# A transformer block kernel: SyncE's queue in the text's order, input halves on ScalarE's queue, x loaded into unused places, and a denser plan for expert weights

## The chip, the cores and the metric

The kernel runs on one core of a Trainium2 chip. The core has TensorE (PE in the rows; PEld is its loading of stationary operands), VectorE (DVE), ScalarE (ACT), GpSimd (POOL) and SyncE (SP), and 16 DMA engines that all the DMA queues share. The metric is the device time of one execution in microseconds (us), and lower is better. The profile of one execution gives the span from the first to the last instruction, which is a little shorter than the device time.

## What is computed

One layer of a streaming encoder over 256 tokens of width 2048, all in float32: a norm, one wide input projection, two parallel mixers (sparse attention with 8 heads, and RWKV-7 with 16 heads), an output projection, and then a mixture of 16 experts, of which each token takes two.

```python
h = rms_norm(x, g_mix[l])
proj = h @ w_in[l]
...
y_dsa = dsa_mixer(q, k, v, q_idx, k_idx, w_idx, q_gain[l], k_gain[l])
y_rwkv = rwkv7_mixer(r, d_w, kr, vr, d_a, d_g, ...)
x = x + jnp.concatenate([y_dsa, y_rwkv], axis=-1) @ w_out[l]
x = x + hier_moe(rms_norm(x, g_ffn[l]), ...)
```

Inside RWKV, a state per head is updated token by token (`state*w + sa*b + v*k`). The kernel does this in chunks of 64 tokens, which needs the solution of small triangular systems.

## The kernel before

The first part is one long stream of weight tasks on TensorE. A task multiplies a 128x512 piece of a weight matrix. `load_raw` brings two such pieces (512 KB) into one of three raw places (RA's two halves and RB) with a DMA on SyncE's queue. `split` then makes a high part (a cast on ACT, L222) and a remainder (a subtraction on DVE, L223), in one of four half buffers W2, and TensorE multiplies three times with the high and low parts of the input (`hT`, or later `yT`). A column task (`add_cm`) is 12 matmuls of 256 columns, a row task (`add_tm`) 6 of 512 columns. `drive` runs the stream: loads are asked for up to 8 tasks ahead, splits 4 tasks ahead.

Between the tasks stand the matmuls of the small chains: the eight RWKV blocks (`rwkv_early`, `solve`, `solved`, `rwkv_late`), the attention, the norm (`spread`). A planner, the class `Order`, decides where: it adds up an estimated TensorE time `od.t`, each chain gives a delay with `yield`, and a step is taken when its due time has come. The table `Y` and the constants `SOLVE_US` and `RSTD_US` hold these delays, and `PACE` the rate at which weights of the experts are asked for while the stream runs. TensorE's instructions keep this order (`manual_schedule`). The order on the other engines, and on SyncE's queue, is decided by the framework's scheduler.

At the start, `xT` (the input, transposed, in four quarters of 512 KB; the first in two halves) and the first raw weights are loaded on SyncE's queue; ACT and DVE make `hT` from `xT` with the gain. The factor 1/rms of a token is needed only when the first projected blocks leave PSUM: `spread` loads x (four pieces of 512 KB, on POOL's queue) into the places of `yr` and `qT`, squares them on ACT into `vt`, and a matmul into `rps` (12 tasks into the stream) spreads the result over the partitions as `rsB`.

`solve` of an RWKV block sends its triangular systems through DRAM to POOL, which solves them row by row (`tt`, `xt`, L692 and L694) and writes `dout`; `solved` loads the result into `XT` with four DMAs on SyncE's queue (L702), and the first matmuls `pz1` of `rwkv_late` read it. `load_lora` brings small weights (128 KB) on SyncE's queue too.

After the mixers, four groups of 16 tasks multiply `wo` (the output projection). During these, `prefetch_step`, `leave_rwkv` and `wo_after` load the first expert weights, in chunks of 1 MB, on POOL's queue; a one-element copy from the current W2 half holds most of them back until the stream has come that far. Then follow the routing and the experts (`experts`), with 24 chunks for each pair of experts and 8 pairs, loaded into a ring of some 23 places.

Of the kernel before, what the change touches and what calls it, by code (L numbers as in the profile page):

```python
# [17 lines left out]
P = 128  # L18
# [17 lines left out]
PACE0 = 8.0  # L36
PACE, SOLVE_US, RSTD_US = 2.2, 39.0, 16.1
Y = [8.0, 5.6, 9.8, 1.6, 4.0, 2.6, 4.8, 5.8, 3.1, 6.0, 5.2, 3.0, 3.0, 3.1, 19.0, 5.7, 12.6, 4.4, 7.2, 4.8, 2.2, 6.6, 2.8, 6.2, 7.2, 2.2, 3.5, 0.0, 1.5, 1.1, 2.2, 16.1, 5.0, 2.2, 10.7, 10.4, 1.0, 5.0]

STREAM = ["r1", "d0", "r2", "d1", "r3", "d2", "r4", "r5", "d4", "r6", "r7", "d3", "d5", "d6", "d7"]

# [89 lines left out]
def block_kernel(ctx: ExitStack, tc: tile.TileContext, a: dict, dbg=None):  # L133
# [23 lines left out]

    ACT.preload_act_table_set("natural_log_exp_and_others")

    const = ctx.enter_context(tc.tile_pool(name="const", bufs=1))  # L160
# [13 lines left out]
    order = ExitStack()  # L174
    order.enter_context(tc.manual_schedule(engines={mybir.EngineType.PE}))

# [79 lines left out]
    with tc.tile_pool(name="xload", bufs=1) as xp:  # L256
# [4 lines left out]
        def load_xT(q, r0, r1):  # L261
            SP.dma_start(out=xT[q][:, r0:r1, :], in_=a["xT"][:, 4 * q + r0:4 * q + r1, :])

# [24 lines left out]
    def spread():  # L288

        yield 4.0  # L290
        part = const.tile([P, 2, 2], F32, name="part")
        xv = a["x"].rearrange("(j p) (c m) -> p j c m", p=P, c=2)
        xs = [t.rearrange("p b t -> p (b t)").rearrange("p (c m) -> p c m", c=2) for t in (yr, qT)]
        for j in range(2):
            for c in range(2):
                POOL.dma_start(out=xs[j][:, c, :], in_=xv[:, j, c, :])
                yield 1.0
        for j in range(2):
            for c in range(2):
                ACT.activation(out=vt[:, j, :], in_=xs[j][:, c, :], func=AF.Square, accum_out=part[:, j, c:c + 1])  # L300
                yield 1.0 * c
        DVE.tensor_tensor(out=rstd, in0=part[:, :, 0], in1=part[:, :, 1], op=ALU.add)
# [252 lines left out]
    def rwkv_early(b):  # L555
# [142 lines left out]
    def solved(b):  # L698

        yield SOLVE_US  # L700
        for ci in range(4):
            tc.keep_in_program_order(SP.dma_start(out=XTs[b % SB][32 * ci:32 * ci + 32, :, 32 * ci:32 * ci + 32], in_=dr[b][1][ci].rearrange("u s t -> s u t")))  # L702
        od.event(f"solved{b}", Y[37])

    def rwkv_late(b):
# [60 lines left out]
        for n in range(1, 3):  # L766
# [871 lines left out]
```

## Time and profile before

| what | value |
|---|---|
| device time, median of 3 runs | 1052.73 us (1046.85 to 1052.93) |
| device time of the profiled execution | 1053.52 us |
| its span | 1051.7 us |
| mean granted clock of TensorE, share of full speed | 0.998 |
| TensorE busy | 1012.2 us (96%) |
| VectorE, ScalarE, GpSimd busy | 528.9, 387.7, 257.8 us |
| moved by DMA | 298.75 MB, mean 284 GB/s |

A row of the timeline gives the start in us from the span's start, the time in us, engine, line, operation, what is written and read, and in square brackets the idle time of the engine before it with what ended it. SPq is SyncE's queue; its rows are issues of DMAs, not transfers. A row of the chain of waits gives start and length, and "DMA RB<-wo" there is a transfer from its issue to its landing. A row of the waits names the engine that waited, what it waited for, the us in total, how often, and the longest.

### The profile page before, as it was taken

The page shows a single profiled execution, that of the slowest core. Times are in us where ns is not written, and L with a number is a line of the kernel's source. Part 1 is how long each engine was busy: PE and PEld are TensorE (multiplying, and loading weights), DVE is VectorE, ACT ScalarE, POOL GpSimd, SP SyncE. Part 2 cuts the span into 40 slices and gives each one's busy share as a digit, 9 for nine tenths or more (in the row PEclk, how much of TensorE's full clock was granted, in tenths as well). Part 3 has the DMA queues.
Part 4 walks back from the last instruction along what each step waited for, and adds up shares of the span by engine and source line. Part 5 has one row for each costly group of instructions (what it writes and reads, how often), then busy time and mean ns, then how long its engine had stood idle before and what let it go on. Part 6 is the DMA issues. An engine that isn't in the chain of part 4 may idle for free.

```text
span 1051.7 us, 17181 instructions
## 1 busy us (share of the span) xinstructions
PE 1012.2 (96%) x6476; PEld 683.2 (65%) x6476; DVE 528.9 (50%) x1155; ACT 387.7 (37%) x836; POOL 257.8 (25%) x645
## 2 busy tenths in 40 slices
PE   5899999999999999999999899999999999999995
PEld 5898888889889877788877544444444444444432
DVE  5696787698978765756554313131312222221303
ACT  5666656566566754566454101010101010000001
POOL 3206676572664737002222110000000000000000
PEclk9999999999999999999999999999999999999999
DMA  8556744535454464648899798999999999999995
GB/s 286 211 180 174 203 150 136 167 114 147 134 155 139 137 189 133 235 123 289 285 324 378 314 365 352 422 419 420 420 421 419 421 420 420 419 421 420 420 405 176
DMA packets 69210, 298.75 MB, mean 284 GB/s; under 512 B 17184, under 2 KB 20048, under 8 KB 45056
## 3 DMA queue, kind: packets, MB, share of 16 engines
q1 hardware_dynamic: 54864, 248.59, 63.6%
q0 software_dynamic: 8928, 47.41, 12.7%
q10 hardware_dynamic: 5328, 1.58, 0.6%
q8 instruction: 53, 0.87, 0.3%
q14 instruction: 37, 0.30, 0.1%
HBM read 294.37 MB, written 3.15 MB: 283 GB/s over the span
## 4 chain that ended last, share of the span: by engine, by line
PE 78%; DVE 8%; DMA 5%; ACT 3%; issue 2%; POOL 2%; SPq 0%; ACTq 0%; DVEq 0%; POOLq 0%
PE pp L146 27%; PE pd L146 11%; PE gate L146 11%; PE up L146 10%; PE misc L146 6%; PE sc L146 3%; DVE W L223 3%; PE pz L146 2%; DMA RB<-wo 2%; PE py L146 2%; DMA RB<-wr 1%; POOL xt L694 1%; ACT W L222 1%; POOL tt L692 1%; DMA xT<-xT 1%
## 5 line engine op out<-in xcount | busy, mean ns | idle before, releaser
L146 PE MATMUL pp<-W,hT 128*128 128x512 f32 x768 | 190.1, 397 | 0.0
L146 PE MATMUL pp<-hT,W 128*128 128x256 f32 x1296 | 170.9, 289 | 11.8 <-DVE W L223 8.4
L223 DVE TENSOR_TENSOR W<-RA,W 128x512 fp32r<-128x512 f32 x200 | 138.3, 701 | 81.6 <-ACT W L222 80.9
L146 PEld LDWEIGHTS pp<-hT,W 128*128 128x128 f32 x1296 | 161.8, 194 | 16.2 <-DVE W L223 9.2
L222 ACT CAST W<-RA 128x512 fp32r<-128x512 f32 x200 | 121.8, 618 | 100.9 <-PE pp L146 52.2
L146 PEld LDWEIGHTS pp<-W,hT 128*128 128x128 f32 x768 | 139.8, 188 | 29.0 <-issue 0.7
L692 POOL TENSOR_TENSOR tt<-xt,at 128x24 f32<-128x24 f32 (+23 forms) x248 | 87.5, 353 | 52.5 <-DMA at<-din 33.7
L694 POOL TENSOR_TENSOR xt<-xt,tt 128x24 f32<-128x24 f32 (+23 forms) x248 | 94.4, 381 | 19.5
L146 PE MATMUL pp<-W,yT 128*128 128x512 f32 x384 | 91.3, 394 | 2.1 <-DVE W L223 2.1
L223 DVE TENSOR_TENSOR W<-RB,W 128x512 fp32r<-128x512 f32 x100 | 69.1, 696 | 48.3 <-ACT W L222 48.1
L146 PE MATMUL pd<-ew,R 128*64 128x512 f32 (+1 forms) x368 | 81.3, 580 | 2.0 <-DVE Y L1482 1.4
L222 ACT CAST W<-RB 128x512 fp32r<-128x512 f32 x100 | 61.2, 618 | 59.1 <-PE pp L146 28.3
L146 PEld LDWEIGHTS pp<-W,yT 128*128 128x128 f32 x384 | 71.0, 188 | 18.4 <-DVE W L223 3.6
L146 PE MATMUL up<-ew,R 128*64 128x512 f32 x352 | 79.3, 592 | 0.0
L146 PEld LDWEIGHTS misc<-sel,uu 128*128 128x128 f32 x512 | 60.1, 191 | 18.8 <-issue 13.8
L1491 ACT ACTIVATE Y<-pd,sv 128x512 fp32r<-128x512 f32 x31 | 21.3, 688 | 134.0 <-PE pd L146 134.0
L146 PE MATMUL misc<-sel,uu 128*128 128x128 f32 x512 | 64.9, 280 | 2.8 <-DVE R L1396 2.1
L1501 DVE TENSOR_TENSOR x<-x,sc 128x512 f32<-128x512 f32 (+1 forms) x58 | 36.2, 666 | 57.3 <-PE sc L146 57.3
L1396 DVE TENSOR_TENSOR R<-misc,gF 128x512 f32<-128x512 f32 x28 | 19.4, 692 | 87.1 <-PE misc L146 87.1
L146 PE MATMUL gate<-ew,R 128*64 128x512 f32 x272 | 61.7, 595 | 0.0
L1492 DVE SCALAR_TENSOR_TENSOR Y<-pd,sv,Y 128x512 fp32r<-128x512 f32 x31 | 23.3, 751 | 73.2 <-ACT Y L1491 73.2
L1420 ACT CAST selT<-misc 128x256 fp32r<-128x256 f32 x8 | 3.0, 372 | 153.7 <-PE misc L146 153.7
(389 smaller groups left out, 1216.4 us busy)
## 6 DMA issues: line engine op xcount, KB each, us to landing
ew<-we SPq DMA_DIRECT2D x66, 1024.0 KB, 19.9
ew<-wdn SPq DMA_DIRECT2D x38, 1024.0 KB, 19.3
ew<-we POOLq DMA_DIRECT2D x25, 1024.0 KB, 7.5
ewh<-we SPq DMA_DIRECT2D x24, 1024.0 KB, 18.2
RA<-wd SPq DMA_DIRECT2D x43, 512.0 KB, 3.8
RA<-wr SPq DMA_DIRECT2D x35, 512.0 KB, 3.9
RB<-wd SPq DMA_DIRECT2D x21, 512.0 KB, 3.7
RA<-wo SPq DMA_DIRECT2D x21, 512.0 KB, 4.6
```

What stands on the lines that cost most here:

```text
L146: PE.matmul(out, lhsT=lhsT, rhs=rhs, start=start, stop=stop, skip_group_check=skip)
L222: ACT.copy(out=hi, in_=raw)
L223: DVE.tensor_tensor(out=lo, in0=raw, in1=hi.bitcast(F32), op=ALU.subtract)
L692: POOL.tensor_tensor(out=tv, in0=xt[:, 0:n, s_:s_ + 1].broadcast_to([P, n, m]), in1=at[s_ >= 8][:, s_ % 8 if s_ < 8 else s_ - 8, s_ + 1:32 ...
L694: POOL.tensor_tensor(out=xt[:, 0:n, s_ + 1:32], in0=xt[:, 0:n, s_ + 1:32], in1=tv, op=ALU.subtract)
L1396: DVE.tensor_tensor(out=t[:, a:b], in0=ps.rearrange("p (a t) -> p a t", t=P)[:, a:b], in1=gF[:, 4 * kq + a:4 * kq + b].rearrange("p (a o) ...
L1420: ACT.copy(out=selT, in_=ps[:, 0:T])
L1491: ACT.activation(out=yh, in_=pd, func=AF.Copy, scale=sv[:, 1:2])
L1492: DVE.scalar_tensor_tensor(out=yl, in0=pd, scalar=sv[:, 1:2], in1=yh.bitcast(F32), op0=ALU.mult, op1=ALU.subtract)
L1501: DVE.tensor_tensor(out=x1[j][:, ns], in0=(uu[:, j, ns] if first else x1[j][:, ns]), in1=ps, op=ALU.add)
```

## The change

SyncE is added to the engines that keep the text's order. The loads of `xT` go to ScalarE's queue, ahead of the load of its table. `spread` loads x at the start: its fourth piece into half of `G[1]`, without any condition, the other three into buffers of the tag `MM` behind a one-element copy that reads the third quarter of `hT`; the squares are written in place. `load_lora` stands at later places in the text. In the planner, `PACE` falls from 2.2 to 1.8, `SOLVE_US` rises from 39 to 42, some delays in `Y` change, and `r4` (RWKV block 4) comes ahead of `d2` in the stream.

```diff
-PACE, SOLVE_US, RSTD_US = 2.2, 39.0, 16.1
-Y = [8.0, 5.6, 9.8, 1.6, 4.0, 2.6, 4.8, 5.8, 3.1, ..., 3.0, 3.1, ..., 12.6, ..., 5.0]
-STREAM = ["r1", "d0", "r2", "d1", "r3", "d2", "r4", "r5", ...]
+PACE, SOLVE_US, RSTD_US = 1.8, 42.0, 16.1
+Y = [8.0, 5.6, 9.8, 2.4, 4.0, 2.6, 4.8, 5.8, 3.4, ..., 3.6, 3.1, ..., 13.2, ..., 4.0]
+STREAM = ["r1", "d0", "r2", "d1", "r3", "r4", "d2", "r5", ...]
...
-    ACT.preload_act_table_set("natural_log_exp_and_others")
...
-    order.enter_context(tc.manual_schedule(engines={mybir.EngineType.PE}))
+    order.enter_context(tc.manual_schedule(engines={mybir.EngineType.PE, mybir.EngineType.SP}))
...
-            SP.dma_start(out=xT[q][:, r0:r1, :], in_=a["xT"][:, 4 * q + r0:4 * q + r1, :])
+            ACT.dma_start(out=xT[q][:, r0:r1, :], in_=a["xT"][:, 4 * q + r0:4 * q + r1, :])
...
+        ACT.preload_act_table_set("natural_log_exp_and_others")
...
-        yield 4.0
...
-        xs = [t.rearrange("p b t -> p (b t)").rearrange("p (c m) -> p c m", c=2) for t in (yr, qT)]
-        for j in range(2):
-            for c in range(2):
-                POOL.dma_start(out=xs[j][:, c, :], in_=xv[:, j, c, :])
-                yield 1.0
-        for j in range(2):
-            for c in range(2):
-                ACT.activation(out=vt[:, j, :], in_=xs[j][:, c, :], func=AF.Square, accum_out=part[:, j, c:c + 1])
-                yield 1.0 * c
+        xs = [state.tile([P, 1024], F32, name="xs", tag="MM", bufs=SB + 1) for _ in range(3)] + [G[1][:, 1024:2048]]
+        POOL.tensor_copy(xs[0][0:1, 0:1], hT[2][0:1, 0, 0, 0:1].bitcast(F32))
+        for n in range(4):
+            POOL.dma_start(out=xs[n], in_=xv[:, n // 2, n % 2, :])
+        yield 10.0
+        for n in range(4):
+            ACT.activation(out=xs[n], in_=xs[n], func=AF.Square, accum_out=part[:, n // 2, n % 2:n % 2 + 1])
+            yield 1.0 * (n % 2)
...
-            load_lora(b + 1, i)
...
-        load_lora(b + 1, 0)
         DVE.tensor_tensor(out=kd, in0=k, in1=di, op=ALU.mult)
         yield Y[2]
+        load_lora(b + 1, 0)
...
-            tc.keep_in_program_order(SP.dma_start(out=XTs[b % SB][...], in_=dr[b][1][ci].rearrange("u s t -> s u t")))
+            SP.dma_start(out=XTs[b % SB][...], in_=dr[b][1][ci].rearrange("u s t -> s u t"))
...
+        load_lora(b + 1, 2)
         od.release("@late")
```

The first place is ACT's queue from the start. hT and W are the high parts, RA and RB the raw weights; a row with x2 stands for two instructions. Before:

```order
L158 ACT_TABLE_LOAD
L285 ACTIVATE hT_68<-xT_110,gT 128x256 x2
L222 CAST W_83<-RA 128x512 x2
L285 ACTIVATE hT_68<-xT_110,gT 128x256 x2
L285 ACTIVATE hT_69<-xT_111,gT 128x256 x4
L222 CAST W_84<-RA 128x512 x2
L285 ACTIVATE hT_70<-xT_112,gT 128x256 x4
```

Now, behind the five DMAs of xT:

```order
L275 ACT_TABLE_LOAD
L284 ACTIVATE hT_67<-xT_109,gT 128x256
L220 CAST W_82<-RA 128x512
L284 ACTIVATE hT_67<-xT_109,gT 128x256 x3
L298 ACTIVATE G_88,part<-G_88 128x1024
L284 ACTIVATE hT_68<-xT_110,gT 128x256 x4
L220 CAST W_82<-RA 128x512
L284 ACTIVATE hT_69<-xT_111,gT 128x256 x4
```

The second cast of W has moved behind the second quarter of hT, and the square of the fourth piece of x (L298) stands between the first two quarters.

The second place is ACT's queue some ten us later, from the cast of RB (tasks 4 and 5 of the stream) on. Before, the squares are the L300 rows:

```order
L222 CAST W_83<-RB 128x512 x2
L498 CAST two_early<-G_89 128x256
L498 CAST lw<-lraw 128x256
L222 CAST W_84<-RA 128x512 x2
L222 CAST W_83<-RA 128x512 x2
L300 ACTIVATE vt,part<-yr 128x1024
L222 CAST W_84<-RB 128x512 x2
L300 ACTIVATE vt,part<-yr 128x1024
L300 ACTIVATE vt,part<-qT 128x1024 x2
L303 ACTIVATE rstd<-rstd,eps_t 128x2
```

Now:

```order
L220 CAST W_82<-RB 128x512 x2
L496 CAST two_early<-G_88 128x256
L496 CAST lw<-lraw 128x256
L220 CAST W_83<-RA 128x512 x2
L298 ACTIVATE xs,part<-xs 128x1024 x3
L301 ACTIVATE rstd<-rstd,eps_t 128x2
L220 CAST W_82<-RA 128x512 x2
L302 ACTIVATE rstd<-rstd 128x2
L220 CAST W_83<-RB 128x512 x2
```

The three remaining squares stand in one run ahead of the casts for tasks 8 to 11, where before one square stood behind those of 8 and 9 and three behind those of 10 and 11.

The third place is the first result of the solve. On SyncE's queue XT<-dout is that load, RA and RB are weights. Before:

```order
L210 DMA RA<-wd 128x1024 x2
L210 DMA RB<-wd 128x1024
L210 DMA RA<-wd 128x1024
L702 DMA XT_186<-dout_198 32x4x32 x4
L210 DMA RA<-wd 128x1024
L210 DMA RB<-wd 128x1024
```

Now:

```order
L208 DMA RB<-wd 128x1024
L208 DMA RA<-wd 128x1024 x2
L699 DMA XT_186<-dout_198 32x4x32 x4
L208 DMA RB<-wd 128x1024
L208 DMA RA<-wd 128x1024
L208 DMA RA<-wr 128x1024
```

The load of XT stands behind one more load of weights. On TensorE, the matmuls that read it (pz<-R,XT), with those ahead of them from the matmuls of `p3` on; before:

```order
L146 MATMUL p_1562<-con,G_89 128x128 x2
L146 MATMUL pp<-W_83,hT_68 128x512 x6
L146 MATMUL pp<-W_84,hT_68 128x512 x12
L146 MATMUL pp<-W_83,hT_69 128x512 x3
L146 MATMUL pz<-X_192,two_early 128x256 x4
L146 MATMUL pb<-Vc,AB 64x64 x8
L146 MATMUL pp<-W_83,hT_69 128x512 x6
L146 MATMUL pz_1640<-R,XT_186 128x128 x4
```

Now (ahead of the first of these rows 12 matmuls of 128x512 stand since the last 256-column task, before it were 6):

```order
L146 MATMUL p_1575<-con,G_88 128x128 x2
L146 MATMUL pp<-W_83,hT_67 128x512 x12
L146 MATMUL pp<-W_82,hT_68 128x512 x12
L146 MATMUL pb<-Vc,AB 64x64 x8
L146 MATMUL pz<-X_192,two_early 128x256 x4
L146 MATMUL pz_1647<-R,XT_186 128x128 x4
```

Since that task there are now 36 matmuls of 512 columns ahead of the reader, where there were 33. Over the eight blocks, 38, 48, 58, 68, 77, 89, 99 and 109 loads of weights stand ahead of XT before, and 39, 49, 59, 68, 77, 89, 99 and 109 now; counted in tasks of the stream, the reader comes 1.5 nearer to its load in the first block and in the third to fifth, and 1 nearer in the second. On POOL's queue, twelve chunks of expert weights instead of eleven stand ahead of the first one that no copy holds back.

## Rows read from the trace of the kernel before

**Rows 1.** The page's head and its first part: span, and TensorE's busy time, share and instructions.

```profile
span 1051.7 us, 17181 instructions
...
PE 1012.2 (96%) x6476; PEld 683.2 (65%) x6476; DVE 528.9 (50%) x1155; ACT 387.7 (37%) x836; POOL 257.8 (25%) x645
```

**Rows 2.** Busy time of the engines by stretch (PE, PEld, DVE, ACT, POOL, each with its instructions), then the granted clock of TensorE, the mean busy share of the DMA engines, and GB/s: the start, the end of the projection, and 100 us of the experts.

```profile
0.00:50.00 50.00, 35.74 (x260) 34.47 (x261) 29.44 (x61) 30.54 (x62) 16.14 (x43) 1.00 0.75 254
...
550.00:600.00 50.00, 44.52 (x248) 33.01 (x248) 21.13 (x66) 15.07 (x33) 10.59 (x22) 1.00 0.87 341
600.00:700.00 100.00, 99.16 (x514) 44.45 (x511) 22.19 (x43) 8.71 (x13) 5.80 (x11) 1.00 0.97 387
```

**Rows 3.** The waits of TensorE's matmuls over the whole span: us in total, times, longest.

```profile
PE pp L146 <- DVE W L223: 10.5, 6, 7.0
PE pp L146 <- ACT hT L285: 3.4, 1, 3.4
PE rps L146 <- DVE G L307: 2.8, 1, 2.8
PE tps L156 <- DVE re L742: 2.2, 1, 2.2
...
PE pz L146 <- DVE R L728: 1.1, 1, 1.1
...
PE pbp L146 <- DVE two_early L499: 0.8, 1, 0.8
```

**Rows 4.** The timeline of the first 36 us, chosen rows.

```profile
0.74 1.28 ACT L158 ACT_TABLE_LOAD   x1 [0.74 <-PEq L1631]
...
1.66 0.90 SPq L210 DMA_DIRECT2D RA<-wr  x2
...
5.61 0.62 ACT L222 CAST W<-RA 128x512 fp32r<-128x512 f32 x1 [0.42 <-DMA RA<-wr]
...
7.00 1.65 PE L146 MATMUL pp<-hT,W 128*128 128x256 f32 x6 [7.00 <-DVE W L223]
...
12.04 7.88 PE L146 MATMUL pp<-hT,W 128*128 128x256 f32 x42 [3.39 <-ACT hT L285]
...
15.41 3.30 ACT L285 ACTIVATE hT<-xT,gT 128x256 fp32r<-128x256 f32 x8
...
18.62 1.13 ACT L222 CAST W<-RB 128x512 fp32r<-128x512 f32 x2
...
19.78 1.06 POOL L296 DMA_DIRECT2D yr<-x  x2 [16.01 <-DMA G<-lora]
...
20.14 8.89 PE L146 MATMUL pp<-hT,W 128*128 128x256 f32 x72 [0.21 <-DVE W L223]
...
21.43 2.51 ACT L222 CAST W<-RA 128x512 fp32r<-128x512 f32 x4 [0.93 <-DMA RA<-wr]
...
28.45 1.14 ACT L222 CAST W<-RB 128x512 fp32r<-128x512 f32 x2 [2.83 <-DMA RB<-wr]
...
29.86 3.13 PE L146 MATMUL pp<-hT,W 128*128 128x256 f32 x24 [0.83 <-DVE W L223]
...
31.71 1.06 ACT L300 ACTIVATE vt<-qT 128x1024 f32<-128x1024 f32 x1
...
35.82 0.67 PE L146 MATMUL rps<-G 128*128 128x256 f32 x2 [2.82 <-DVE G L307]
```

**Rows 5.** The same columns as Rows 2 for two stretches of 3 us in the start.

```profile
6.00:9.00 3.00, 1.65 (x6) 1.35 (x6) 0.69 (x1) 0.23 (x1) 0.00 (x0) 1.00 1.03 241
...
12.00:15.00 3.00, 2.96 (x13) 2.83 (x14) 2.70 (x7) 2.62 (x7) 0.00 (x0) 1.00 1.03 411
```

**Rows 6.** The timeline where the first solve's result is loaded and read.

```profile
121.93 0.33 SPq L210 DMA_DIRECT2D RA<-wd  x1
...
122.35 1.99 SPq L702 DMA_DIRECT2D XT<-dout  x4
...
125.19 0.35 SPq L210 DMA_DIRECT2D RA<-wd  x1
...
129.64 1.05 PE L146 MATMUL pz<-R,XT 128*128 128x128 f32 x8
```

**Rows 7.** The view of the tile XT: from the issue to the landing of its 32 DMAs.

```profile
DMA to landing us min/median/max: 3.7/6.3/7.9
```

**Rows 8.** The timeline of the fifth block: the load of XT and its reader.

```profile
291.34 1.81 SPq L702 DMA_DIRECT2D XT<-dout  x4
...
301.48 0.72 PE L146 MATMUL pz<-R,XT 128*128 128x128 f32 x5
```

**Rows 9.** The chain of waits at the end of the projection: two of the last loads of wo.

```profile
557.13 7.92 DMA RB<-wo
...
567.12 9.30 DMA RB<-wo
```

**Rows 10.** The view of the DMAs: issues, KB of each, and the median from issue to landing.

```profile
RB<-wo SPq DMA_DIRECT2D x11, 512.0 KB, 4.7
```

**Rows 11.** The timeline at the same place: the last matmuls of the projection.

```profile
573.35 3.01 PE L146 MATMUL pp<-W,yT 128*128 128x512 f32 x12 [0.50 <-DVE W L223]
...
577.93 1.65 PE L146 MATMUL pp<-W,yT 128*128 128x512 f32 x6 [1.57 <-DVE W L223]
```

**Rows 12.** The waits of SyncE's queue over the whole span.

```profile
SPq L210 <- DVE W L223: 345.1, 120, 7.5
```

More of the change, by code (lines that the diff above doesn't have):

```diff
@@ L36 @@
 PACE0 = 8.0
-PACE, SOLVE_US, RSTD_US = 2.2, 39.0, 16.1
-Y = [8.0, 5.6, 9.8, 1.6, 4.0, 2.6, 4.8, 5.8, 3.1, 6.0, 5.2, 3.0, 3.0, 3.1, 19.0, 5.7, 12.6, 4.4, 7.2, 4.8, 2.2, 6.6, 2.8, 6.2, 7.2, 2.2, 3.5, 0.0, 1.5, 1.1, 2.2, 16.1, 5.0, 2.2, 10.7, 10.4, 1.0, 5.0]
-STREAM = ["r1", "d0", "r2", "d1", "r3", "d2", "r4", "r5", "d4", "r6", "r7", "d3", "d5", "d6", "d7"]
+PACE, SOLVE_US, RSTD_US = 1.8, 42.0, 16.1
+Y = [8.0, 5.6, 9.8, 2.4, 4.0, 2.6, 4.8, 5.8, 3.4, 6.0, 5.2, 3.0, 3.6, 3.1, 19.0, 5.7, 13.2, 4.4, 7.2, 4.8, 2.2, 6.6, 2.8, 6.2, 7.2, 2.2, 3.5, 0.0, 1.5, 1.1, 2.2, 16.1, 5.0, 2.2, 10.7, 10.4, 1.0, 4.0]
+STREAM = ["r1", "d0", "r2", "d1", "r3", "r4", "d2", "r5", "d4", "r6", "r7", "d3", "d5", "d6", "d7"]
 class Order:
@@ L621, in rwkv_early @@
         AB = state.tile([P, 2, 4, 64], F32, name="AB", bufs=SB)
-        MM = state.tile([P, 2, 4, 2, 64], F32, name="MM", bufs=SB + 1)
+        MM = state.tile([P, 2, 4, 2, 64], F32, name="MM", tag="MM", bufs=SB + 1)
         pas = [pbank("pa") for _ in range(2)]
@@ L701, in solved @@
         for ci in range(4):
-            tc.keep_in_program_order(SP.dma_start(out=XTs[b % SB][32 * ci:32 * ci + 32, :, 32 * ci:32 * ci + 32], in_=dr[b][1][ci].rearrange("u s t -> s u t")))
+            SP.dma_start(out=XTs[b % SB][32 * ci:32 * ci + 32, :, 32 * ci:32 * ci + 32], in_=dr[b][1][ci].rearrange("u s t -> s u t"))
         od.event(f"solved{b}", Y[37])
```

## The prediction

> **What bounds the kernel now.** I read the page's head first: TensorE is busy for 96% of the span [rows 1], so the sum can only come from its 40 us of idle time, or from new idle time. The stretches say where that lies: 14.3 of the first 50 us, 5.5 of the 50 us at the end of the projection, and under 1 us of 100 in the experts [rows 2]. The clock is at its full 2.4 GHz level in all three, so it is no term. The experts are therefore out of the sum: their chunks are in another place in the plan, but TensorE's work there is the same. That leaves the waits [rows 3]: the largest are for the split of weights (10.5 us), for hT (3.4), for the matmul of rstd (2.8) and for a few planned chains (2.2, 1.1, 0.8).
>
> The timeline of the start shows which they are [rows 4]. TensorE begins at 7.00 us, six matmuls later it waits 3.39 us for hT, at 29.86 it has waited 0.83 us for a split, and at 35.82 it has waited 2.82 us for rstd. What lies behind the last two: POOL issues x only at 19.78; the last of its squares on ACT begins at 31.71; and RB's weights keep ACT idle for 2.83 us, since they share the DMA engines with x.
>
> **The change, part by part.**
>
> *The input on ScalarE's queue.* The first weights are now issued behind one small load only. One issue on SyncE's queue is 0.45 us (0.90 for two, [rows 4]), so the first split, which follows the cast at 5.61, can be 0.45 us earlier; the table's load (1.28 us) behind five such issues ends at about 0.74 + 5 x 0.45 + 1.28 = 4.3 us, before that cast. Gain at most 0.4.
>
> The 3.39 us wait will not just go. Half a quarter of xT no longer queues behind two pieces of weights, but ACT's new order casts the second piece of W after four more hT, so TensorE stops for that instead. What counts is when the cast of RB (tasks 4 and 5) is done. Before, ACT runs without a break from 15.41 to 18.62 + 1.13 = 19.75. Best case: the 3.39 us are gained. Worst: the early piece of x, 0.5 MB, moves everything back; at the 411 GB/s of the second stretch in [rows 5] that is 1.3 us. I take a gain of 0.8 for the first five tasks, nearer the worst, as ACT also has 1.06 us more to do there, a square.
>
> *x early.* The copy that holds back three pieces reads a part of hT that is written at about 15.4, so they are issued 4.4 us before the 19.78 of now, and are 0.5 MB less (1.3 us). The last square could then begin at 31.71 - 5.7 = 26.0. Nothing waits for rstd any more, but the new order puts three squares in one run (3 x 1.06, so 3.2 us) ahead of the casts for tasks 8 and 9. If the last begins at 26.0, they end at 27.1; with a cast (0.62, as at 5.61) and a subtraction that I take to be as long, task 8 is ready at 28.4. Before, TensorE came to task 8 at about 25.9: 20.14 plus 48 matmuls of 0.12 (8.89 us for 72). With the gain of 0.8 it comes at 25.1 and waits 3.3 us. Tasks 8 to 11 then run in 5.8 us without a wait, to 34.2, against 35.82. If x lands sooner, the squares follow the first two of the casts of RA from 21.43 on (2.51 us for four), begin at 22.7, end at 25.9, and TensorE is there at 33.0. So the start as a whole gains 1.6 to 2.8; I take 2.0, with bounds at a loss of 1.3 (above) and a gain of 7.0 (3.39 + 0.83 + 2.82, all gone).
>
> *SyncE in the text's order.* Its queue waits 345 us for free raw places [rows 12], so it is ahead of what it feeds, and the small loads at later places cost and bring nothing; without that cover each would delay a load of weights by its issue, 0.33 us [rows 6]. What matters is XT. In the first block it was issued at 122.35 and read at 129.64, 7.3 us later, without a wait [rows 6]. Now it stands behind one more load, that of 125.19, so it is issued at about 125.6. The reader moves by three matmuls of 0.25 us (3.01 us for 12, [rows 11]), to 130.4, which leaves 4.8 us. A DMA of XT takes 3.7 to 7.9 us, 6.3 in the middle [rows 7], and the last one is issued some 1.5 us after the first. So TensorE waits 0.4 (if 5.2 suffices) to 2.5 us (if 7.3 are needed); I take 2.0, since the middle lies nearer to the long end. In the fifth block 10.1 us lie between them [rows 8]; 1.5 tasks less (2.2 us) leave 7.9, which is enough, and the third and fourth I take to be like it, the others keep their place.
>
> *Delays in the plan.* Three of the longer waits in [rows 3] have their delay raised: pbp 0.8 us (raised by 0.8), pz 1.1 (by 0.3), tps 2.2 (by 0.6). I count 0.8 + 0.3 + 0.6 = 1.7 as gained. Bounds: none of it, or all 4.1. The block that changes place with a projection brings the same tasks, so I count it at nothing; it is covered by the four tasks that are split ahead, and costs a wait like those three, 0.8 to 2.2 us, where a chain then comes too late.
>
> *Expert weights in closer sequence.* At the end of the projection two loads of wo take 7.92 and 9.30 us [rows 9], against 4.7 in the middle [rows 10], and TensorE waits 0.50 and 1.57 us for their splits [rows 11]. One chunk of 1 MB now goes ahead of that crowd: at 411 GB/s it is 2.5 us less there. I take a gain of 1.5, between 2.1 (both gone) and a loss of 1.0 if the denser sequence slows a load of wo earlier, where the trace shows no wait.
>
> The sum: -2.0 (start) + 2.0 (XT) - 1.7 (delays) - 1.5 (end of the projection) = -3.2 us on a span of 1051.7. Around the span of that execution lie 1053.52 - 1051.7 = 1.8 us, so the time is 1048.5 + 1.8 = 1050.3, say 1050; the median of the runs, 1052.73, is 0.8 below the profiled one.
>
> **The rivals.**
>
> First: the start gives all it has. If x is squared before TensorE comes to task 8 and the second quarter is there early, the 7.0 us go and not 2.0: 1050 - 5 = 1045. For it speaks that the ACT rows hold no long wait for DMA but those of the weights; against it that ACT has the same casts and more squares before task 8.
>
> Second: the start gives nothing, because three queues share the same engines. In the stretch from 6 to 9 us these are fully busy at only 241 GB/s [rows 5], while POOL's small loads are under way. A 0.5 MB piece on POOL's queue then delays xT by its 1.3 us, and the start loses 1.3 where I count 2.0 won: 1050 + 3.3 = 1053, so no change. The Trainium skill, DMA: Bandwidth & Descriptors, section Issuing engines are not separate DMA queues, speaks for this one: by it DMAs of several engines run on the same 16 and interleave, and only the time of issuing is saved. The busy share in that stretch agrees; no row here shows three queues at once.
>
> Third, the slower one: XT comes too late in every block. Its place is now fixed by the plan, and the plan knows nothing of how long its DMA takes. If every block had only the 4.8 us of the first, at 7.9 us per load that is 3.1 x 8 = 25 us; half of it, 12, gives 1050 + 12 = 1062. It decides from the point at which more than two blocks have under 7.3 us between issue and reader. Against it: no load of XT stands more than one load of weights later than now, and no reader comes more than 1.5 tasks nearer.
>
> **How the numbers follow.** The forecast, 1047 to 1053, gets 0.50; the first rival 0.15; the second 0.20; the third, or another chain too late, 0.15. The likeliest is the first of these, so 1050. For the range I go out to the first rival with the delays' upper bound (1045 - 2.4, so 1043) and to most of the third (1059): about 8 in 10. A measurement can tell about 1%, 10.5 us, from no change. Over 1% faster (under 1042) would need all the waits of the start, all of the delays and of the end of the projection at once: 0.10. Over 1% slower (over 1063) is the upper part of the third rival: 0.08. Within: 0.82.
>
> **What would show it.** In the changed kernel's profile: no wait of rps for DVE, and one of 2 to 4 us for a split near task 8, between 24 and 30 us; TensorE at the rstd matmul at about 34; the first block's pz preceded by up to 2.5 us of idle time that a DMA of XT ends; the last loads of wo at 6 to 8 us and under 1 us of waits for their splits. It would be wrong if ACT waits long for the first square of x at 8 to 12 us (the start then loses), if pz waits in more than two blocks, or if SyncE's queue waits for dout with weights behind it.

## The result, and the profile after

The changed kernel takes 1063.93 us (median of 4, 1060.37 to 1064.67), beside 1052.83 us of the kernel before on the same chip: ratio 1.011, 95% interval 1.0064 to 1.0155, so about 11 us slower. The profiled execution took 1064.67 us, its span is 1062.9 us.

The page's head and first part of the kernel after:

```profile
span 1062.9 us, 17143 instructions
...
PE 1016.4 (96%) x6476; PEld 688.0 (65%) x6476; DVE 527.9 (50%) x1155; ACT 387.9 (36%) x836; POOL 256.8 (24%) x646
```

Against [rows 1] the span is 11.2 us longer, and TensorE is busy 4.2 us longer with the same 6476 matmuls. So two things happened: 7.0 us more idle time, and 4.2 us because the same work ran slower. The stretches say where the clock fell (columns as in [rows 2]):

```profile
0.00:50.00 50.00, 33.64 (x235) 33.09 (x236) 27.58 (x58) 29.33 (x60) 17.21 (x44) 0.90 0.70 236
50.00:150.00 100.00, 97.17 (x706) 87.40 (x706) 78.90 (x162) 59.98 (x127) 48.26 (x124) 0.98 0.60 174
...
350.00:450.00 100.00, 96.87 (x699) 78.36 (x699) 68.64 (x160) 60.25 (x142) 50.85 (x136) 0.98 0.59 174
...
550.00:600.00 50.00, 44.58 (x239) 34.54 (x238) 21.58 (x57) 19.47 (x40) 9.93 (x21) 1.00 0.97 382
600.00:700.00 100.00, 98.21 (x519) 47.37 (x520) 22.16 (x53) 7.49 (x12) 7.36 (x14) 0.98 0.88 350
```

TensorE has 33.64 us of work in the first 50 us instead of 35.74 [rows 2], at a mean clock of 0.90. The end of the projection is as it was (44.58 and 44.52), with the DMA engines now at 0.97 of their time instead of 0.87. The waits of TensorE's matmuls over the whole span (total, times, longest):

```profile
PE pp L146 <- DVE W L221: 21.7, 6, 7.6
PE pz L146 <- DMA XT<-dout: 6.3, 4, 2.8
```

The waits for splits have doubled [rows 3], those for the load of XT are new, and the ones for hT, rstd, tps and pbp are gone.

By the place in the program: TensorE's first matmul of wo starts at 482.2 us before and 491.8 now, its last ends at 581.7 and 591.8, and the first matmul of the experts starts at 594.1 and 605.6. So 9.6 of the 11.2 us are lost ahead of the projection with wo (3.1 of them by the rstd matmul), 0.5 in it, 1.4 between it and the experts, and none in the experts.

The start, timeline of the first 40 us, chosen rows (ACTq is ScalarE's DMA queue):

```profile
0.74 3.60 ACTq L260 DMA_DIRECT2D xT<-xT  x5
...
4.38 1.28 ACT L275 ACT_TABLE_LOAD   x1 [4.38 <-DMA xT<-xT]
...
7.61 2.93 PE L146 MATMUL pp<-hT,W 128*128 128x256 f32 x12 [7.61 <-DVE W L221]
...
12.90 1.06 ACT L298 ACTIVATE G<-G 128x1024 f32<-128x1024 f32 x1 [4.87 <-DMA G<-x]
...
13.96 1.69 ACT L284 ACTIVATE hT<-xT,gT 128x256 fp32r<-128x256 f32 x4
...
15.55 0.60 ACT L220 CAST W<-RA 128x512 fp32r<-128x512 f32 x1
...
16.87 1.59 POOL L295 DMA_DIRECT2D xs<-x  x3
...
16.93 12.31 PE L146 MATMUL pp<-hT,W 128*128 128x256 f32 x84 [6.40 <-DVE W L221]
...
31.60 7.51 PE L146 MATMUL pp<-hT,W 128*128 128x256 f32 x48 [2.35 <-DVE W L221]
...
38.96 0.60 PE L146 MATMUL rps<-G 128*128 128x256 f32 x2
```

Beside [rows 4]: the table's load ends at 5.66 us, since the five issues ahead of it took 3.60 us, 0.72 for each where I had counted 0.45. Then ACT stands still for 4.87 us with the square of the early piece of x at the head of its queue; the second quarter of hT and the second piece of W are behind it. TensorE stops at 10.5 and goes on at 16.93. From there it runs at half clock, and again behind the wait of 2.35 us at 31.60 (windows of 3 and 4 us):

```profile
9.00:12.00 3.00, 1.54 (x8) 1.24 (x6) 0.00 (x0) 0.00 (x0) 0.00 (x0) 1.00 1.03 418
...
15.00:18.00 3.00, 1.06 (x5) 1.07 (x6) 2.98 (x8) 3.00 (x8) 1.37 (x4) 0.50 0.79 281
18.00:21.00 3.00, 3.00 (x16) 3.00 (x16) 3.00 (x8) 3.00 (x8) 2.25 (x3) 0.50 1.04 272
...
31.00:35.00 4.00, 3.40 (x16) 3.40 (x17) 2.75 (x6) 1.99 (x5) 0.00 (x0) 0.59 0.39 120
```

At 0.50 the clock is at its lower level, 1.2 GHz. Before the change TensorE waited 3.39 us at this place, and the clock stayed up [rows 2, 4]. The rstd matmul comes at 38.96 us instead of 35.82.

The load of XT, timeline of the first and the fifth block, and the view of the tile:

```profile
126.64 1.81 SPq L699 DMA_DIRECT2D XT<-dout  x4
...
134.70 1.62 PE L146 MATMUL pz<-R,XT 128*128 128x128 f32 x6 [2.76 <-DMA XT<-dout]
```

```profile
298.79 2.04 SPq L699 DMA_DIRECT2D XT<-dout  x4
...
308.54 1.13 PE L146 MATMUL pz<-R,XT 128*128 128x128 f32 x8 [1.61 <-DMA XT<-dout]
```

```profile
DMA to landing us min/median/max: 2.4/6.8/9.1
```

In the first block the reader could have started 5.3 us after the first issue (134.70 - 2.76 - 126.64), and the four loads took 8.1. In the fifth it is 8.1 us, and they took 9.7. Before, the reader came 7.3 and 10.1 us behind the first issue [rows 6, 8]. The other two waits stand in the fourth block (1.16 us) and the sixth (0.73). The first of the waits is followed by another stretch at half clock, and so is one for a split at 420 us (that wait, the windows behind the two, and one more between the projection and the experts):

```profile
423.02 1.20 PE L146 MATMUL pp<-W,hT 128*128 128x512 f32 x4 [2.38 <-DVE W L221]
```

```profile
134.00:137.00 3.00, 2.30 (x10) 2.23 (x11) 1.98 (x5) 0.73 (x3) 2.45 (x8) 0.52 0.42 90
424.00:427.00 3.00, 3.00 (x38) 2.02 (x39) 1.75 (x4) 0.62 (x1) 1.34 (x3) 0.54 0.95 373
...
600.00:610.00 10.00, 9.05 (x49) 6.37 (x50) 3.23 (x15) 0.17 (x1) 1.01 (x2) 0.83 0.30 106
```

In the last of these windows no wait is long: TensorE's two longest idle times there are 1.14 and 0.73 us.

At the end of the projection, the view of the DMAs (median us from issue to landing) and the last matmuls:

```profile
RA<-wo SPq DMA_DIRECT2D x21, 512.0 KB, 5.9
...
RB<-wo SPq DMA_DIRECT2D x11, 512.0 KB, 6.3
```

```profile
578.00 3.02 PE L146 MATMUL pp<-W,yT 128*128 128x512 f32 x12 [1.92 <-DVE W L221]
...
588.00 1.66 PE L146 MATMUL pp<-W,yT 128*128 128x512 f32 x6 [1.09 <-DVE W L221]
```

A load of wo into RB takes 6.3 us instead of 4.7 [rows 10]. TensorE has two waits here of 1.92 and 1.09 us, where it had 0.50 and 1.57 [rows 11]; the first of them comes four tasks earlier than the 0.50 did.

### The profile page after: what moved, and what is told of

The parts are those of the page before. It is cut to its first block, busy times and chain, and to the rows that moved or that the text cites. A ratio compares the mean times of both kernels' runs of the same rounds, so it can differ in the third digit from the quotient of the medians.

```text
span 1062.9 us, 17143 instructions
## 1 busy us (share of the span) xinstructions
PE 1016.4 (96%) x6476; PEld 688.0 (65%) x6476; DVE 527.9 (50%) x1155; ACT 387.9 (36%) x836; POOL 256.8 (24%) x646
## 4 chain that ended last, share of the span: by engine, by line
PE 66%; DMA 14%; POOL 7%; DVE 6%; issue 3%; ACT 2%; ACTq 0%; SPq 0%; POOLq 0%; DVEq 0%
PE pp L146 24%; PE gate L146 9%; PE up L146 9%; PE pd L146 8%; PE misc L146 6%; POOL tt L689 3%; POOL xt L691 3%; PE sc L146 3%; DMA XT<-dout 3%; DMA ew<-wdn 2%; DMA ew<-we 2%; DMA eww<-we 2%; PE pz L146 2%; DVE W L221 2%; DMA at<-din 2%
## 5 line engine op out<-in xcount | busy, mean ns | idle before, releaser
L691 POOL TENSOR_TENSOR xt<-xt,tt 128x24 f32<-128x24 f32 (+23 forms) x248 | 91.6, 369 | 19.5
L146 PEld LDWEIGHTS misc<-sel,uu 128*128 128x128 f32 x512 | 61.5, 195 | 18.8 <-issue 13.8
```

What stands on the lines that cost most here:

```text
L146: PE.matmul(out, lhsT=lhsT, rhs=rhs, start=start, stop=stop, skip_group_check=skip)
L691: POOL.tensor_tensor(out=xt[:, 0:n, s_ + 1:32], in0=xt[:, 0:n, s_ + 1:32], in1=tv, op=ALU.subtract)
```

## The experiments

Eighteen kernels, each timed together with the kernel before. In the table, "rstd" is the start of the rstd matmul in the profile, "XT" the waits of TensorE for the load of XT (us, times), "splits" its waits for splits from 450 to 600 us, "wo" the median landing of the loads of wo into RA and RB.

| kernel | us | ratio to before (95%) | rstd | XT | splits | wo |
|---|---|---|---|---|---|---|
| before | 1052.7 | 1 | 35.8 | 0 | 2.1, 2 | 4.6, 4.7 |
| the change | 1063.9 | 1.0110 (1.0064-1.0155) | 39.0 | 6.3, 4 | 3.0, 2 | 5.9, 6.3 |
| `s1_old_start` | 1062.9 | 1.0125 (1.0085-1.0165) | 38.1 | 5.6, 3 | 1.9, 1 | 5.6, 5.8 |
| `s2_new_start_alone` | 1055.1 | 1.0013 (0.9988-1.0039) | 39.5 | 1.8, 1 | 1.5, 1 | 5.6, 4.8 |
| `s3_square_late` | 1059.8 | 1.0090 (1.0055-1.0126) | 36.6 | 4.9, 3 | 1.9, 1 | 5.6, 5.9 |
| `s4_x_all_late` | 1063.1 | 1.0101 (1.0068-1.0133) | 35.5 | 7.2, 4 | 3.9, 3 | 5.6, 6.1 |
| `m1_old_numbers` | 1053.3 | 0.9998 (0.9975-1.0021) | 37.2 | 0.9, 2 | 0.4, 1 | 4.8, 4.8 |
| `m2_reader_later` | 1059.3 | 1.0057 (1.0032-1.0083) | 39.1 | 0.9, 1 | 5.7, 4 | 6.5, 5.8 |
| `m3_pace` | 1061.3 | 1.0086 (1.0061-1.0111) | 36.9 | 4.5, 3 | 2.0, 3 | 4.9, 4.8 |
| `m4_sp_alone` | 1052.0 | 0.9995 (0.9969-1.0022) | 34.6 | 0 | 0 | 5.1, 4.3 |
| `n1_xt_pair` | 1069.6 | 1.0138 (1.0106-1.0171) | 40.2 | 5.0, 3 | 4.1, 7 | 6.6, 6.1 |
| `n2_pace` | 1058.1 | 1.0036 (1.0013-1.0058) | 38.4 | 1.8, 2 | 3.0, 2 | 5.1, 4.9 |
| `n3_delays` | 1063.1 | 1.0082 (1.0050-1.0114) | 37.2 | 6.7, 3 | 0.7, 1 | 4.7, 4.5 |
| `n4_stream` | 1058.7 | 1.0044 (1.0020-1.0067) | 36.7 | 0.5, 1 | 1.2, 1 | 5.5, 5.1 |
| `f1_load_earlier` | 1066.3 | 1.0119 (1.0098-1.0140) | 36.8 | 2.1, 1 | 7.8, 6 | 6.5, 7.3 |
| `f2_pair_back` | 1067.6 | 1.0129 (1.0112-1.0147) | 36.6 | 5.5, 2 | 4.9, 3 | 5.4, 6.4 |
| `f3_base_square_late` | 1052.2 | 0.9990 (0.9974-1.0006) | 37.5 | 1.7, 2 | 0.3, 1 | 4.9, 4.3 |
| `f4_three_out` | 1054.7 | 1.0032 (1.0009-1.0054) | 37.3 | 1.3, 1 | 0 | 4.9, 4.5 |
| `g1_earlier_pace` | 1059.1 | 1.0064 (1.0036-1.0092) | 38.5 | 1.8, 1 | 3.0, 3 | 5.9, 5.0 |
| `g2_earlier_square` | 1064.1 | 1.0107 (1.0067-1.0146) | 36.4 | 0.2, 1 | 7.6, 7 | 6.9, 6.9 |

0.1% is 1.05 us. Differences between kernels of different rows are taken from the ratios.

### The start

My theory after reading the profile: start and middle lose apart from each other, 3 us and 8 us.

`s1_old_start`, the start's hunks reversed:

```diff
-            ACT.dma_start(out=xT[q][:, r0:r1, :], in_=a["xT"][:, 4 * q + r0:4 * q + r1, :])
+            SP.dma_start(out=xT[q][:, r0:r1, :], in_=a["xT"][:, 4 * q + r0:4 * q + r1, :])
...
-        xs = [state.tile([P, 1024], F32, name="xs", tag="MM", bufs=SB + 1) for _ in range(3)] + [G[1][:, 1024:2048]]
+        xs = [t.rearrange("p b t -> p (b t)").rearrange("p (c m) -> p c m", c=2) for t in (yr, qT)]
```

> The changed kernel with the whole start of before: xT on SyncE's queue, the table first, x on POOL's queue into yr and qT, squares into vt. Theory A (start and middle lose apart from each other, and the sum is what was measured): the rstd matmul is back at about 35.8 us instead of 38.96, the granted clock stays at its upper level in the first 40 us, the four waits of pz for XT remain, and the time is 1064 - 3.1 = 1061, or 1059 if the half-clock stretches in the start cost more on top. Rival B (the start is the whole loss, because all later chains run against a stream that is late): 1053. Rival C (the start's loss is made good later, the middle is everything): 1064.

Not so: the ratio is 1.0125, no better than the change. TensorE waits 5.2 us for rstd in it, and the middle loses as before. `s2_new_start_alone` has the same hunks the other way round, in the kernel before.

> The kernel before with the new start alone; SyncE's order, delays, stream and loads of lora as before. Theory A: the rstd matmul at about 39 us, 3 us late, and 1053 + 3 = 1056 (up to 1058). Rival B: 1064. Rival C: 1053.

1.0013: the new start costs 1.4 us at the middle of its interval, which holds zero. So the start is not where the 11 us are, although the rstd matmul is 3.7 us late in this profile too.

`s3_square_late`: the early piece stays early, its square waits.

```diff
+        one = const.tile([P, 1], F32, name="one")
+        POOL.tensor_scalar(one, hT[2][:, 0, 0, 0:1].bitcast(F32), 0.0, 1.0, ALU.mult, ALU.add)
...
-            ACT.activation(out=xs[n], in_=xs[n], func=AF.Square, accum_out=...)
+            ACT.activation(out=xs[n], in_=xs[n], func=AF.Square, scale=one if n == 3 else 1.0, accum_out=...)
```

> The changed kernel, but the square of the early piece of x also takes as its scale a column of ones that is written once the third quarter of hT is there; so the piece is still loaded early, and only its square stands later in ACT's queue. Theory A1 (the square at the head of ACT's queue is what stops the start): the second quarter of xT landed at 9.25 us, so its hT ends at about 11 instead of 15.6, TensorE's wait of 6.4 us falls to 2 or 3 with a second one for the next weights, the clock stays up, and the rstd matmul comes 2 to 3 us earlier, at 36 to 37; time about 1061. Rival A2 (the 512 KB ahead of xT are what cost): the wait of 6.4 us shrinks by less than 1.3, and the time stays at 1063.

The timeline of its start, chosen rows:

```profile
9.48 1.71 ACT L284 ACTIVATE hT<-xT,gT 128x256 fp32r<-128x256 f32 x4 [1.24 <-DMA xT<-xT]
...
12.47 1.71 PE L146 MATMUL pp<-hT,W 128*128 128x256 f32 x12 [1.74 <-DVE W L221]
...
16.14 4.02 PE L146 MATMUL pp<-hT,W 128*128 128x256 f32 x24 [1.96 <-DVE W L221]
...
36.63 0.59 PE L146 MATMUL rps<-G 128*128 128x256 f32 x2
```

As theory A1 has it, hT of the second quarter begins at 9.48 and not at 13.96, TensorE goes on at 12.47, the one wait of 6.40 us is now 1.74 and 1.96, and the clock stays at 1.00 in the first 40 us. The order in ACT's queue moved hT and shortened the wait, since the bytes are loaded as before. For the clock this isn't shown: with the square late as well, it is 0.96 in `f4_three_out` and `g2_earlier_square`. In all twelve profiles with the square early this wait is 5.2 to 6.4 us and ends at 16.6 to 17.1 us; in the four with it late TensorE goes on at 12.1 to 13.8. The Trainium skill, PSUM — Partial Sum Buffer, section Engine vs sequencer instructions, calls ScalarE's queue a strict FIFO; the 4.87 us in the timeline after agree. Most of that is spent again on the way: the rstd matmul comes at 36.6 to 40.2 us in the twelve, at 36.4 to 37.5 in the four, 1.1 us earlier on the mean. The time gains 0.2% by the ratios, less than either interval. `s4_x_all_late` holds back the piece itself:

```diff
+        POOL.tensor_copy(xs[3][0:1, 0:1], hT[2][0:1, 0, 0, 0:1].bitcast(F32))
```

> The changed kernel, but the early piece of x is held back by the same copy as the other three, so no byte of x is ahead of xT and its square is late as well. Theory A1: hardly better than the kernel in which only the square is late, 0 to 1.3 us (the 512 KB at 411 GB/s), and then a loss where the last piece of x lands later. Rival A2: all of the start's loss of 3 us is undone by this one and not by that one; 1061 against 1063.

The rstd matmul comes at 35.5, 3.5 us earlier than in the change, and the time hardly moves (1.0101): the middle gives it back, with 7.2 us for XT and 3.9 for splits.

### The numbers or the order

`m1_old_numbers` is the change with PACE, SOLVE_US, Y and STREAM of before:

```diff
-PACE, SOLVE_US, RSTD_US = 1.8, 42.0, 16.1
+PACE, SOLVE_US, RSTD_US = 2.2, 39.0, 16.1
...
```

> The changed kernel with PACE, SOLVE_US, Y and STREAM of before; SyncE in the text's order, the new places of the loads of lora and the new start stay. The new start alone cost 2 us. Theory N (the numbers lose the middle: the reader of XT stands 4 us of planned time behind its load instead of 5, and r4 ahead of d2): the waits for XT shrink to one of 2 us in the first block, the wait for W at 420 us goes, and the time is 1053 + 2 = 1055 to 1057. Theory Q (SyncE's fixed order loses it, whatever the numbers): three or four waits for XT stay, 5 to 6 us, and the time is 1061 to 1064.

0.9998. With the old numbers the loss is gone, and SyncE's order with the new start costs nothing that can be measured. No run puts the new numbers into the kernel with the old order, so whether they lose without SyncE's order isn't shown. `m4_sp_alone` is the kernel before with SyncE's order and the new places of `load_lora` (their hunks are left out here):

```diff
-    order.enter_context(tc.manual_schedule(engines={mybir.EngineType.PE}))
+    order.enter_context(tc.manual_schedule(engines={mybir.EngineType.PE, mybir.EngineType.SP}))
```

> The kernel before with SyncE's queue in the text's order and the loads of lora at their new places; start and numbers as before. Theory N: 1053, with no waits for XT. Theory Q: 5 to 6 us of waits for XT in three or four blocks, 1058 to 1060. A start that is late by 2 us at the rstd matmul, as in the kernel with the old start, is expected of either, since the squares and the casts stand as there.

0.9995, without one wait for XT: by itself the order costs nothing that can be measured. I had expected its rstd matmul late; it is early, at 34.6.

Two numbers of the change, set one at a time. `m2_reader_later` puts the reader of XT 8 us behind its load, where before the change it was 5:

```diff
-Y = [..., 4.0]
+Y = [..., 8.0]
```

> The changed kernel with one number: the reader of XT is planned 8 us behind its load instead of 4. From first issue to last landing the load took 3.8 to 9.6 us. If the waits for XT (6.3 us in four) and the stretch at half clock behind the first of them (1.7 us) are what the middle loses: no wait for XT of over 1 us, and 1064 - 8 = 1056. If the chains only end later and something else waits: 1061 to 1064.

XT is no longer waited for (0.9 us), and 5.6 us of the time come back, not 8: the splits now wait 5.7 us at the end of the projection. `m3_pace`:

```diff
-PACE, SOLVE_US, RSTD_US = 1.8, 42.0, 16.1
+PACE, SOLVE_US, RSTD_US = 2.2, 42.0, 16.1
```

> The changed kernel with PACE 2.2 as before. If the denser loading of expert weights costs at the end of the projection and where a one-element copy on POOL holds a W2 half (2.4 us at 420 us): 1064 - 2 to -4 = 1060 to 1062. If PACE is worth nothing either way: 1064.

Loads of wo are back at 4.9 and 4.8 us. By the ratios 2.5 us of the time come back too, which is less than the change's own interval.

### One number at a time on the old ones

The base is `m1_old_numbers`. `n1_xt_pair` sets SOLVE_US 42 and the reader's delay 4, `n2_pace` PACE 1.8, `n3_delays` the four raised delays, `n4_stream` puts r4 ahead of d2 (one hunk each, in this order):

```diff
-PACE, SOLVE_US, RSTD_US = 2.2, 39.0, 16.1
-Y = [..., 5.0]
+PACE, SOLVE_US, RSTD_US = 2.2, 42.0, 16.1
+Y = [..., 4.0]
...
-PACE, SOLVE_US, RSTD_US = 2.2, 39.0, 16.1
+PACE, SOLVE_US, RSTD_US = 1.8, 39.0, 16.1
...
-Y = [8.0, 5.6, 9.8, 1.6, ..., 3.1, ..., 3.0, 3.1, ..., 12.6, ...]
+Y = [8.0, 5.6, 9.8, 2.4, ..., 3.4, ..., 3.6, 3.1, ..., 13.2, ...]
...
-STREAM = ["r1", "d0", "r2", "d1", "r3", "d2", "r4", "r5", ...]
+STREAM = ["r1", "d0", "r2", "d1", "r3", "r4", "d2", "r5", ...]
```

> The changed kernel with PACE, Y and STREAM of before (1053.3 us), but SOLVE_US 42 and the reader of XT 4 us behind its load, as in the change. Theory P (this pair makes the load of XT late, and is about half of the loss): three or four waits for XT, 4 to 6 us, perhaps a stretch at half clock, and 1053 + 5 = 1058. If XT is late only together with r4 ahead of d2 or the other delays: no waits for XT, 1053.

> The same base (1053.3 us) with PACE 1.8 alone. From the run with PACE 2.2 in the changed kernel: 1053 + 2.7 = 1056, lost in waits for splits of wo, at 525 to 580 us, and not at the waits for XT. My prediction's step counted 1.5 us as gained here: 1052.

> The same base with the four raised delays alone (2.4, 3.4, 3.6 and 13.2). My prediction's step counted 1.7 us as gained: the waits pbp, pz for R and tps go, 1051.6. If chains that come later only run into others: 1053 or 1054.

> The same base with r4 ahead of d2 alone. My prediction counted it at nothing: 1053. The parts of the loss so far (XT pair and its clock 4.6, PACE 2.7, start 2.3 of 11) leave 1.5 to 3 us over; if they are here: 1055 to 1056, with waits in the blocks from 140 to 310 us.

Each costs: 1.4%, 0.4%, 0.8% and 0.5%, that is 15, 4, 9 and 5 us. Together, in the change, they cost 11. So they don't add up, and none has a price of its own. The waits of TensorE in `n1_xt_pair` and in `n3_delays`:

```profile
PE pz L146 <- DMA XT<-dout: 5.0, 3, 2.7
...
PE tps L156 <- DVE qo L879: 3.1, 1, 3.1
```

```profile
PE pz L146 <- DMA XT<-dout: 6.7, 3, 4.6
```

In `n3_delays` neither the load of XT nor its reader has another number, yet there is a wait of 4.6 us for it in the first block: 5.5 us lie between the first issue and the place of the reader, where the base has 7.4 with the same planned delay, and the reader starts 10.1 us after that issue, where the base's starts after 7.9. The other chains' delays have moved the stream against the load, and the load takes longer there. In `n4_stream` XT is not late at all, and tps waits 4.1 us.

### The load of XT on its own, and three causes together

`f1_load_earlier` leaves the reader where the change has it and asks for the load 3 us earlier; `f2_pair_back` has the pair as before the change.

```diff
-PACE, SOLVE_US, RSTD_US = 1.8, 42.0, 16.1
-Y = [..., 4.0]
+PACE, SOLVE_US, RSTD_US = 1.8, 39.0, 16.1
+Y = [..., 7.0]
```

> The changed kernel with the load of XT planned 3 us earlier and its reader where the change put it (SOLVE_US 39, delay of the reader 7: the sum is 46 as in the change). In SyncE's queue 38, 48, 58, 67, 76, 87, 99 and 110 loads of weights stand ahead of XT. The solve's result is in DRAM 4.5 us or more before the load is issued, so nothing new has to be waited for. Theory P (the lateness of the load is what the pair costs): no wait for XT over 1 us, 1064 - 6.3 - 1.7 = 1056. Theory M (any other place of the chains costs elsewhere, since the plan fits one set of numbers only): the waits for XT go, others come, 1059 to 1063.

> The changed kernel with SOLVE_US 39 and the reader 5 us behind its load, as before the change; PACE, the four delays, the stream, the start as in the change. The same loads stand ahead of XT as in the kernel with the load earlier, and the reader is planned 2 us earlier. Theory P: one or two waits for XT of 1 to 2 us, 1058. Theory M: other waits come, 1060 to 1066, as the delays alone on the old numbers cost 9 us.

My theory P fell. In `f1_load_earlier` only the first block waits for XT (2.1 us), the stream comes to the 1800th matmul of the weights 7.6 us earlier than in the change, and the kernel is no faster (1.0119). `f2_pair_back` is no faster either (1.0129), with a wait of 4.5 us for XT in the first block. In `f1_load_earlier` TensorE needs 109.0 us from the first matmul of wo to the last, where the change needs 100.0. The chain of waits at the end of the projection, and the landing of the loads of wo, show where the gain went:

```profile
509.31 9.55 DMA RA<-wo
...
539.31 8.84 DMA RA<-wo
...
550.23 8.76 DMA RA<-wo
...
561.06 9.08 DMA RA<-wo
```

```profile
RA<-wo SPq DMA_DIRECT2D x21, 512.0 KB, 6.5
...
RB<-wo SPq DMA_DIRECT2D x11, 512.0 KB, 7.3
```

```profile
PE pp L146 <- DVE W L221: 7.8, 6, 2.1
```

Loads of wo of nearly 9 us stand in that chain, and TensorE waits 7.8 us for splits. The time that was gained ahead of the projection was lost again inside it. `f4_three_out` takes PACE and the early square away as well, `g1_earlier_pace` and `g2_earlier_square` one of the two; `f3_base_square_late` is `m1_old_numbers` with the square late. For `f4_three_out`, beside the hunk of `s3_square_late`:

```diff
-PACE, SOLVE_US, RSTD_US = 1.8, 42.0, 16.1
-Y = [..., 4.0]
+PACE, SOLVE_US, RSTD_US = 2.2, 39.0, 16.1
+Y = [..., 7.0]
```

> The changed kernel without the three causes so far: square late (4.1 us in its own run), PACE 2.2 (2.7), load of XT 3 us earlier with the reader where it is (8 if theory P holds). If they add up: 1064 - 4 - 2.7 - 8 = 1049. If theory M holds: 1056 to 1060, since the four delays and r4 ahead of d2 stay.

> The changed kernel with the load of XT 3 us earlier (its reader in place) and PACE 2.2; the start as in the change. With PACE 1.8 this was 1066.3, with 8.4 us of waits for splits of wo at 517 to 580 us. If PACE is what loses the end of the projection: these waits shrink to 1 us or none, and 1066 - 8 = 1058. If the square is what the kernel with all three taken out gained: 1063 to 1066.

> The same earlier load of XT and the early square late, PACE 1.8 as in the change. If PACE loses the end of the projection: its waits stay at 5 to 8 us, and 1066 - 2 to -4 = 1062 to 1064. If the square alone brings the 11.6 us: 1055.

> PACE, SOLVE_US, Y and STREAM of before, SyncE in the text's order, the new start with the early square late. If what that square costs is the same here as in the changed kernel (there 4 us): 1053.3 - 2 to -4 = 1049 to 1051, with the rstd matmul near 36 and no half clock in the first 40 us; the one candidate that may beat both kernels. If not: 1053.

Page and loads of wo of `f4_three_out` (this profiled execution is its shortest, the median is 1054.7):

```profile
span 1048.0 us, 17137 instructions
...
PE 1014.2 (97%) x6476; PEld 686.3 (65%) x6476; DVE 530.0 (51%) x1155; ACT 387.9 (37%) x836; POOL 258.9 (25%) x647
```

```profile
RA<-wo SPq DMA_DIRECT2D x21, 512.0 KB, 4.9
...
RB<-wo SPq DMA_DIRECT2D x11, 512.0 KB, 4.5
```

With all three out the loss is 0.3% instead of 1.1%, and the projection takes 95.9 us. From `f1_load_earlier`, PACE alone brings 0.55%, the square alone 0.12%, both 0.87%. PACE 1.8 against 2.2 stands in four pairs: the change and `m3_pace` 0.24%, `m1` and `n2` 0.38%, `f1` and `g1` 0.55%, `g2` and `f4` 0.75%, so it costs 2.5 to 7.9 us, each time with more waits for splits; the smallest of the four is within its intervals. The late square stands in four pairs as well: 0.20, 0.08, 0.12 and 0.32%, each within its intervals, all of the same sign. None of the kernels is shown to beat the one before; `f3_base_square_late` comes nearest, 0.9990 with an interval that holds 1.

## Why the prediction was wrong

It said 1050 us, 3 faster; it is 11 slower. Its terms one by one:

- **SyncE's order at nothing:** right (`m4_sp_alone`, -0.05%).
- **The start, a gain of 2.0:** wrong in sign, small in size. It is 0.1% slower alone. The step that failed is "I take a gain of 0.8 for the first five tasks": it counted the square as 1.06 us of work on ACT and not as a wait for its data at the head of the queue. The text had named that wait as what would make it wrong. The three pieces that were held back, put at 15.4 us, went at 16.87, behind the late hT. Two of the signs that it named came: no wait of rps, and one of 2.35 us for the split of task 8; but the rstd matmul came at 38.96 us, not at 34. The "gain at most 0.4" for the first weights was a loss as well: the issues on ACT's queue put the table's load off to 5.66 us, and TensorE began at 7.61 and not at 7.00. The second rival (start gives nothing, 1053) is what `s2_new_start_alone` and `m1_old_numbers` measured, but not by its mechanism: the bytes that it blamed are as early in `s3_square_late`, which has not the long wait.
- **XT, 2.0 in the first block only:** there the distance was nearly right (4.8 us foreseen, 5.3 measured), and so was the wait (2.76). The term failed in the other blocks, in two steps. "1.5 tasks less (2.2 us) leave 7.9, which is enough": in the fifth block the distance was 8.1, but the last of the four DMAs came 9.7 us after the first issue; the load was sized by single DMAs of 3.7 to 7.9 us [rows 7] and by the 7.3 us that had been enough before. And "the third and fourth I take to be like it, the others keep their place": the place among the loads of weights does not fix the time. The distance fell from 11.2 to 6.9 us in the third block, from 10.8 to 6.9 in the fourth, and in the sixth, with no task less, from 10.3 to 7.8. So four blocks waited, 6.3 us, and four had less than 7.3 us. That is the third rival's mechanism, with half of the 12 us that it counted, and its point of decision, more than two blocks, was passed.
- **The delays, a gain of 1.7:** wrong in sign on the old numbers: 9 us lost. The waits of tps and pbp are gone in the change, as foreseen; the step that failed is "I count 0.8 + 0.3 + 0.6 = 1.7 as gained", which lets each of them go without moving anything else.
- **r4 ahead of d2 at nothing:** 5 us lost on the old numbers, with a wait of 4.1 us for tps where the base has 1.5.
- **Expert weights in closer sequence, a gain of 1.5:** wrong in sign; 2.5 to 7.9 us lost in all four pairs. The step was "One chunk of 1 MB now goes ahead of that crowd: at 411 GB/s it is 2.5 us less there." One chunk did leave the last quarter of the projection (in its four quarters 4, 2, 5 and 6 are issued, before 4, 1, 5 and 7; by its end 20 in either kernel), but the loads of wo got no faster for it: their medians are 0.1 to 2.4 us longer with PACE 1.8 in the four pairs. Which chunk delays which load isn't shown.
- **The clock, "no term":** 4.2 us of the 11.2 in the profiled execution. I read it from a trace that has no such stretch, and costed no new stall at more than its length. That trace was a lucky one: its mean granted clock is 0.998, while the 105 executions of the same kernel beside the experiments have 0.991 to 0.998, 0.995 on the mean, and the four of the change 0.988 to 0.992.

Behind these stands one step that all terms share: each edit was costed on the trace of before with everything else in place. The runs show that the numbers of the plan hold together. Take the load of XT: undoing its pair alone in the change gives no gain, and doing it alone on the old numbers loses 15 us.

What stays open: why the pair costs 15 us by itself, while all the numbers together cost 11. The profile of `n1_xt_pair` is 15.8 us longer than that of its base: 5.2 us are slower work, and of the 10.6 of idle time 4.1 are for XT and 6.2 for splits; that the pair makes the splits late is seen, and not why. Open too is the last 0.3% of `f4_three_out`, which still has the four delays and the new place of r4. No run takes these two out of the changed kernel, and none has the new numbers without SyncE's order.

## What to carry to other kernels

A hand-tuned table of delays is one object: a new set of numbers has to be timed as a set, since single ones cost here up to more than the whole, and a stall taken out ahead of a stretch that waits for its loads came back inside it. For a transfer in several DMAs, compare the reader's distance with the last landing after the first issue, not with the median of one DMA. An early load into a free place can still stop an engine, if its consumer stands early in that engine's queue: here for 4.87 us, of which the kernel's time showed 0.1 to 0.3%, within the intervals.

## What the runs showed of the hardware that was not expected

- The length of a stall did not tell whether TensorE's granted clock would fall. In the changed kernel's profile it went to its lower level at stalls of 6.40, 2.35, 2.76 and 2.38 us, and at 602 us where the idle times were 1.14 and 0.73 us; in the kernel before it did not at those of 3.39 and 2.82 us [rows 2, 4]. And it isn't the same each time: of the twelve profiles with the square early, all with the stall of 5.2 to 6.4 us, the clock fell at that stall in two (the change and `m3_pace`), in five only at the next stall, of 2.3 to 3.6 us at 31 to 32 us, and in five not at all in the first 40 us. The 4.2 us of slower work are therefore one execution's; in `g1_earlier_pace` TensorE is busy for 1012.6 us, in `f1_load_earlier` for 1017.9.
- The same start ends at different times: in those twelve the first matmul begins at 7.6 to 8.8 us and the rstd matmul at 36.6 to 40.2.
- From 6 to 9 us the DMA engines moved 395 GB/s with input on three queues, where [rows 5] have 241 for the same stretch, at nearly the same busy share (1.01 and 1.03). The Trainium skill, DMA: Bandwidth & Descriptors, section Issuing engines are not separate DMA queues, says that DMAs of several engines share the same 16; a share near 1 in both kernels agrees. What was moved differs as well, and the kernel before reaches 411 GB/s from 12 to 15 us [rows 5], so the queues are not shown to be the reason.
